# Planned durations of attention and recurrence steps corrected in a build-time instruction order, and one gate scale moved from GpSimd to ScalarE

## The chip, the cores and the metric

The kernel runs on one core of one Trainium2 chip. The metric is the device time of one execution in microseconds (us). Before the change three runs took 2851.94 to 2858.27 us, with a median of 2855.22 us. The engines are named as in the profile: PE is TensorE (PEld its weight loads), DVE is VectorE, ACT is ScalarE, POOL is GpSimd, SP is SyncE, which issues the DMAs.

## The reference

One layer of an encoder works on 2048 tokens of 1024 features, all in float32. What it computes, cut short:

```python
xn   = rms_norm(x, mix_norm_g)
aq, ak, av, mq, mk, mv, mo, ipre, fpre, ga, gm = split(xn @ w_in)
att  = chunk_band_attention(aq, ak, av, rel_bias)   # 8 heads of 64, own chunk of 64 + 8 before
mq, mk = silu(causal_conv4(mq, mk))
hm   = mlstm_chunkwise(mq, mk, mv, ipre + b_i, fpre + b_f)   # 4 heads of 128
hm   = rms_norm(hm per head) * mh_norm_g
m    = sigmoid(mo) * hm
y    = sigmoid(ga) * (att @ w_att_proj) + sigmoid(gm) * (m @ w_mlstm_proj)
x    = x + y @ w_out
x    = x + square(relu(rms_norm(x, ffn_norm_g) @ w_up)) @ w_down
out  = rms_norm(x, final_norm_g)
```

In attention each row of scores is a softmax over at most 640 keys; the recurrence is an mLSTM with exponential input gates, a running maximum and a normalising denominator.

## The kernel before

**Arithmetic.** A float32 product is made of three matmuls in the fp32r format: every operand is split into a rounded part and a rest (`split`, L960 on; weights in `split_now`, L423 on), and high x high, high x low and low x high are added up in PSUM (`mm3`, L486 on). A split is one ACT copy and one DVE subtraction, so each 128x512 activation tile and each 128x1024 weight tile costs both engines a pass. Large products are also done by a seven-product scheme on 2x2 blocks (`quad` at L549, with sums made beforehand by `sum_w` and `quad_w` and combined by `combine`, L1756 on).

**Stages.** The tokens are four blocks of 512. Blocks 0 and 1 come first, one after the other: projections, attention and recurrence are interleaved with the dense matmuls (`dense`, L632 on). Then one gate and the output projection of blocks 0 and 1 and the input projections of blocks 2 and 3 are made in the seven-product scheme. Attention and recurrence of blocks 2 and 3 (`attention_far`, `recurrence_far`) run beside the end of the first feed-forward's up projection and its down projection (`down`, L605 on), whose tiles `take_u1` (L2116) loads from DRAM and splits. `project` (L747) is put ahead of the fourth (for block 2) and of the seventh (for block 3) of the down projection's seven products: it waits until all eight mixing tiles of its block are there.

**The program order.** The order of instructions is not written by hand. Every piece of work is a Python generator, a thread of the class `Flow` (L95 on). Before it issues an instruction it yields the engine and a planned duration in ns; `Flow.run` keeps a planned clock for each engine and always takes the ready thread that can start first, at a tie the one of higher priority. A planned end of a step sets the engine's clock and, with a latency by pair of engines (`LAT`), when the thread's next step may be planned. A third value, where there is one, is added to the time of the result and not to the clock of the engine. A matmul step of any thread but the dense one is planned 800 ns (`SLACK`) after its operands. Buffers (PSUM banks, probability tiles, operand tiles) are handed out by the same planned times. The order that comes out is fixed: on the chip each engine runs its list in order, and waits on semaphores where an operand isn't there. The planned durations change nothing in any instruction; they change which one comes next.

The planned durations are formulas of the width:

```python
def act_ns(n, ps=False, ap=0):
    return (51 if ps else 93) + 0.834 * n + 93 * ap
def dve_ns(n):
    return 70 + 1.042 * n
def dve2_ns(n):
    return 70 + 0.55 * n
```

**The steps that the change touches.** In `scores` (L1243 on), for 128 queries of one head: the score matmuls (L1255) in two halves of up to 320 keys; for each half a DVE pass that adds the bias, negates and keeps the row minimum (L1261, followed by a read of the accumulator); a 128x1 minimum of the two (L1267); Exp with row sum on ACT (L1270, again with a read of its accumulator); a reciprocal (L1272); and the scaling of the probabilities, on DVE (L1275), or in blocks 2 and 3 on ACT (L1277) if that engine can start first. `turn` (L1280 on) transposes the probabilities (L1289) and splits them (L1292 on ACT, L1294 on DVE); `weigh` multiplies them by the values (L1220) and stores them in the block's mixing tiles (L1230 to L1239). In `gates_rest` seven steps of a running maximum over 128 positions (L1395). In `rec_out` the row sum of squares for the head norm (L1665). In `evac_og` (blocks 0 and 1) a Tanh of the output gate on ACT (L1544) and then (tanh + 1) times half the head's gain on POOL (L1547). Blocks 2 and 3 already do the latter on ACT (L1950). POOL also sets the two masked corners of each bias tile (L1149, L1150) and takes the -1/2 powers of the norms (L1621).

Of the kernel before, what the change touches and what calls it, by code (L numbers as in the profile page):

```python
# [26 lines left out]
AF = mybir.ActivationFunctionType  # L27
ALU = mybir.AluOpType
# [66 lines left out]
class Flow:  # L95
# [7 lines left out]
               act=dict(pe=220.0, act=130.0, dve=130.0, pool=180.0),  # L103
               dve=dict(pe=220.0, act=130.0, dve=130.0, pool=155.0), pool=dict(pe=290.0, act=130.0, dve=60.0),
# [68 lines left out]
    def run(self):  # L173
        while self.ready or self.blocked:
            moved = True
            while moved:
                moved = False
                for th in sorted(self.blocked, key=lambda x: (x.prio, x.n)):
                    ok, value = self._grant(th)
                    if ok:  # L180
                        self.blocked.remove(th)
                        self.now = th.at
                        self._step(th, value)
                        moved = True
            if not self.ready and not self.blocked:
                break
            if not self.ready:
                raise RuntimeError("no thread can go on")
            best = None
            for th in self.ready:  # L190
                t, frm = th.at
                for e in th.req[0].split("|"):
                    prio = th.prio
                    if e[-1] == "!":
                        e, prio = e[:-1], -1
                    start = t + self.LAT[frm].get(e, 0.0)
                    if e == "pe" and th.prio < 5:
                        start += self.SLACK
                    key = (max(self.clock[e], start), prio, th.n)
                    if best is None or key < best[0]:  # L200
                        best = (key, th, e)
            (start, _, _), th, e = best
            self.ready.remove(th)
            end = start + th.req[1]
            self.clock[e] = end
            if len(th.req) > 2:
                end += th.req[2]
            th.at = self.now = (end, e)
            self._step(th, e)
# [12 lines that stand above are left out]
# [3 lines left out]
class Layer:  # L225
# [1017 lines left out]
    def scores(self, b, i, k, q, bias, sct, ev):  # L1243
        fl, nc = self.fl, self.nc
        e, st = sct
        f = 4 if b == 0 else i
        n = (i + 5 - f) * P
        kf = k.rearrange("p a c -> p (a c)")
        halves = 2 if n > 256 else 1
        w = n // halves  # L1250
        bks = yield "get", self.banks, halves
        yield "pe", 500
        for x in range(halves):
            for y in range(2):
                nc.tensor.matmul(bks[x][:, :w], q[:, y, i * P:(i + 1) * P],  # L1255
                                 kf[:, f * P + x * w:f * P + x * w + w], start=y == 0, stop=y == 1)
        br = bias[:, ::-1]
        j0 = 640 - n
        for x in range(halves):
            yield "dve", dve_ns(w)  # L1260
            nc.vector.tensor_tensor_reduce(  # L1261
                out=e[:, x * w:x * w + w], in0=bks[x][:, :w], in1=br[:, j0 + x * w:j0 + x * w + w],
                op0=ALU.add, op1=ALU.min, scale=-1.0, scalar=3e38, accum_out=st[:, x:x + 1])
            fl.put(self.banks, bks[x])
        if halves == 2:
            yield "dve", 75
            nc.vector.tensor_tensor(st[:, 0:1], st[:, 0:1], st[:, 1:2], op=ALU.min)  # L1267
        mx = st[:, 0:1]
        yield "act", act_ns(n, ap=2)
        nc.scalar.activation(e[:, :n], e[:, :n], AF.Exp, scale=-1.0, bias=mx, accum_out=st[:, 2:3])  # L1270
        yield "dve", 75
        nc.vector.reciprocal(st[:, 3:4], st[:, 2:3])  # L1272
        e0 = yield ("act|dve" if b > 1 else "dve"), 60 + dve2_ns(n)
        if e0 == "dve":
            nc.vector.tensor_scalar(e[:, :n], e[:, :n], st[:, 3:4], None, op0=ALU.mult)  # L1275
        else:
            nc.scalar.mul(e[:, :n], e[:, :n], st[:, 3:4])  # L1277
        fl.set(ev)
# [69 lines left out]
    def gates_rest(self, b, bk):  # L1348
        fl, nc, B, sm = self.fl, self.nc, self.blk[b], self.sm
# [8 lines left out]
        e, d, s, s2, p = (sm[n] for n in ("e", "d", "s", "s2", "p"))  # L1358
# [32 lines left out]
        V.tensor_copy(a[:, 64:], bk[:16, 128:256])  # L1391
        sh = 1
        while sh < P:
            yield "dve", 150
            V.tensor_tensor(z[:, 64:], a[:, 64:], a[:, 64 - sh:192 - sh], op=ALU.max)  # L1395
            a, z = z, a
            sh *= 2
# [3 lines left out]
                         start=True, stop=True)  # L1401
# [137 lines left out]
    def evac_og(self, b, h, bk):  # L1539
        fl, nc, B = self.fl, self.nc, self.blk[b]  # L1540
        yield "wait", [B["ctx_ev"][h]]
        dst = B["ctx"][h][2][:, :512]
        yield "act", act_ns(512, True)
        nc.scalar.activation(dst, bk, AF.Tanh, scale=0.5)  # L1544
        fl.put_dense(self.banks, bk)
        yield "pool", 670
        nc.gpsimd.tensor_scalar(dst, dst, 1.0, self.ghead[:, h:h + 1], op0=ALU.add, op1=ALU.mult)  # L1547
        fl.set(B["og_ev"][h])

    def rec_head(self, b, h):  # L1550
# [105 lines left out]
    def rec_out(self, n, bk, nd, hs, c, ev):  # L1656
        fl, nc = self.fl, self.nc
        yield "act", act_ns(129, True, 1)
        nc.scalar.mul(nd, bk[:, 260:389], self.ex[:, 1, n:n + 1])
        yield "dve", dve_ns(129)  # L1660
        nc.vector.tensor_add(nd, bk[:, 0:129], nd)
        fl.put(self.banks, bk)
        (tmp,) = yield "get", self.temp, 1
        yield "act", act_ns(128, False, 1)
        nc.scalar.activation(tmp[:, :P], nd[:, :P], AF.Square, accum_out=hs[:, 2, c:c + 1])  # L1665
        fl.put(self.temp, tmp)
        fl.set(ev)
# [793 lines left out]
```

## Time and profile before

| what | value |
|---|---|
| median of 3 runs | 2855.22 us |
| the profiled execution | 2851.86 us |
| its span, first to last instruction | 2850.1 us |
| PE busy | 2806.0 us (98%) |
| DVE busy | 2022.0 us (71%) |
| ACT busy | 1579.1 us (55%) |
| POOL busy | 47.3 us (2%) |
| chain that ended last | PE 81%, DVE 7%, DMA 5%, ACT 4% |

The profile is of one execution. A row of a group names the line of the code, the engine, the operation, the tiles written and read, the shapes and the count; after the bar come busy us, the mean ns of one, and the idle time of the engine before them with what ended it. A row of waits says who waited for whom, with the sum in us, the times and the longest. A row of a stretch gives the busy time of PE, PEld, DVE, ACT and POOL (with counts), the granted clock, and the DMA share and rate. The end of a matmul is modelled and lies after the start of the next one, so PE reads as busy for some time in which it could already have started another.

### The profile page before, as it was taken

The numbers are of one execution on the slowest core, as the hardware profiler recorded it, in microseconds if no ns is written. First come the engines' busy times: TensorE is split into PE (matmuls) and PEld (weight loads), VectorE is DVE, ScalarE is ACT, GpSimd is POOL, SyncE is SP. The second block draws the span as 40 slices with busy tenths as digits, with TensorE's granted clock in tenths as the row PEclk, the third lists the DMA queues.
The fourth block names the chain that finished last, engine by engine and source line by source line (L and its number), as shares of the span: only waits on it lengthen the run. The fifth ranks groups of instructions, "written<-read, shape, count | busy, mean of one in ns | idle before, by whom it ended". The sixth has DMA issues, their size and how long they took to land.

```text
span 2850.1 us, 39045 instructions
## 1 busy us (share of the span) xinstructions
PE 2806.0 (98%) x13576; PEld 2343.9 (82%) x13576; DVE 2022.0 (71%) x3750; ACT 1579.1 (55%) x2734; POOL 47.3 (2%) x116
## 2 busy tenths in 40 slices
PE   8999999999999999999999999999999999999998
PEld 7888888888878888878888887888878888888887
DVE  6886479878896867865666787788886744455565
ACT  4664366755444545665456776566545655555444
POOL 0000000000000000000000000000000000000000
PEclk9999999999999999999999999999999999999999
DMA  6327732357765768487888866866677655566563
GB/s 215 99 93 253 247 110 92 119 201 244 258 214 193 237 231 295 165 270 270 299 283 277 257 210 192 242 194 207 222 259 257 211 198 195 200 235 213 187 224 134
DMA packets 276005, 605.74 MB, mean 213 GB/s; under 512 B 30688, under 2 KB 45152, under 8 KB 275808
## 3 DMA queue, kind: packets, MB, share of 16 engines
q1 hardware_dynamic: 275808, 603.26, 63.1%
q8 instruction: 106, 1.74, 0.2%
q14 instruction: 91, 0.75, 0.1%
HBM read 426.98 MB, written 176.16 MB: 212 GB/s over the span
## 4 chain that ended last, share of the span: by engine, by line
PE 81%; DVE 7%; DMA 5%; ACT 4%; issue 1%; POOL 0%; SPq 0%; POOLq 0%; DVEq 0%; ACTq 0%
PE bank L571 36%; PE bank L488 11%; PE bank L489 11%; PE bank L490 11%; PE bank L599 2%; DMA r<-u 2%; PE bank L1220 2%; DVE wsp L429 2%; PE bank L1255 1%; PE bank L1289 1%; ACT wsp L427 1%; DMA wsum<-ctx 1%; DMA ctx<-in_wf 1%; ACT r L963 1%; DVE r L1294 1%
## 5 line engine op out<-in xcount | busy, mean ns | idle before, releaser
L571 PE MATMUL bank<-r,wsp 128*128 128x512 f32 x5208 | 1189.9, 390 | 8.3 <-DVE ctx L1775 6.8
L571 PEld LDWEIGHTS bank<-r,wsp 128*128 128x128 f32 x5208 | 976.9, 188 | 214.3 <-DVE ctx L1775 9.0
L429 DVE TENSOR_TENSOR wsp<-wraw,wsp 128x1024 fp32r<-128x1024 f32 x461 | 562.9, 1221 | 343.0 <-ACT wsp L427 326.1
L427 ACT CAST wsp<-wraw 128x1024 fp32r<-128x1024 f32 x461 | 484.2, 1051 | 464.4 <-PE bank L571 186.9
L488 PE MATMUL bank<-r,wsp 128*128 128x512 f32 x1600 | 640.4, 400 | 0.9 <-ACT r L1237 0.5
L490 PE MATMUL bank<-r,wsp 128*128 128x512 f32 x1600 | 625.1, 391 | 0.0
L489 PE MATMUL bank<-r,wsp 128*128 128x512 f32 x1600 | 624.7, 390 | 0.0
L490 PEld LDWEIGHTS bank<-r,wsp 128*128 128x128 f32 x1600 | 300.3, 188 | 64.8
L488 PEld LDWEIGHTS bank<-r,wsp 128*128 128x128 f32 x1600 | 301.0, 188 | 53.3 <-ACT r L1237 1.0
L489 PEld LDWEIGHTS bank<-r,wsp 128*128 128x128 f32 x1600 | 301.3, 188 | 51.4
L1775 DVE TENSOR_TENSOR ctx<-bank,ctx 128x512 f32<-128x512 f32 x174 | 118.9, 687 | 86.9 <-PE bank L571 86.9
L968 DVE TENSOR_TENSOR r<-r 128x512 fp32r<-128x512 f32 x224 | 149.7, 687 | 37.1 <-ACT r L963 36.1
L963 ACT CAST r<-r 128x512 fp32r<-128x512 f32 x224 | 136.7, 622 | 69.2 <-DMA r<-u 65.4
L1767 ACT COPY ctx<-bank 128x512 f32<-128x512 f32 x174 | 101.1, 582 | 67.7 <-PE bank L571 61.3
L1270 ACT ACTIVATE sc<-sc,scs 128x640 f32<-128x640 f32 (+4 forms) x128 | 97.2, 760 | 70.9 <-DVE scs L1267 68.5
L396 DVE TENSOR_TENSOR ctx<-ctx,ctx 128x512 f32<-128x512 f32 x112 | 76.7, 688 | 70.7 <-DMA ctx<-in_wf 55.5
L2134 ACT ACTIVATE ctx<-ctx 128x512 f32<-128x512 f32 x96 | 60.6, 632 | 107.4 <-DVE ctx L1775 107.1
L1261 DVE CUSTOM_DVE_ANT_0 sc<-bank,bias 128x320 f32<-128x320 f32 (+3 forms) x240 | 104.9, 459 | 15.6 <-PE bank L1255 12.8
L1220 PE MATMUL bank<-r,r 128*128 128x256 f32 (+1 forms) x672 | 110.5, 285 | 5.5 <-DVE r L1294 4.3
L1220 PEld LDWEIGHTS bank<-r,r 128*128 128x128 f32 x672 | 99.2, 191 | 18.8 <-DVE r L1294 9.0
L1294 DVE TENSOR_TENSOR r<-bank,r 128x512 fp32r<-128x512 f32 (+1 forms) x168 | 96.0, 594 | 12.4 <-ACT r L1292 11.6
L1292 ACT CAST r<-bank 128x512 fp32r<-128x512 f32 (+1 forms) x168 | 81.1, 517 | 14.7 <-PE bank L1289 12.8
(276 smaller groups left out, 2888.9 us busy)
## 6 DMA issues: line engine op xcount, KB each, us to landing
wraw<-in_wf SPq DMA_DIRECT2D x170, 512.0 KB, 4.2
wraw<-wsum SPq DMA_DIRECT2D x136, 512.0 KB, 4.0
r<-u SPq DMA_DIRECT2D x224, 256.0 KB, 3.9
wraw<-in_w SPq DMA_DIRECT2D x104, 512.0 KB, 3.9
u<-ctx SPq DMA_DIRECT2D x128, 256.0 KB, 2.6
ctx<-in_wf SPq DMA_DIRECT2D x112, 256.0 KB, 4.3
wsum<-ctx SPq DMA_DIRECT2D x112, 256.0 KB, 3.7
u<-tmp SPq DMA_DIRECT2D x96, 256.0 KB, 3.2
```

Source lines behind the costliest of these rows:

```text
L427: nc.scalar.copy(w[:, 0], raw)
L429: nc.vector.tensor_sub(w[:, 1], raw, w[:, 0].bitcast(F32))
L488: mm(ps, lh, rh, start=first, stop=False)
L489: mm(ps, lh, rl, start=False, stop=False)
L490: mm(ps, ll, rh, start=False, stop=last)
L571: mm(ps, wv[:, x, k, n], a[:, y], start=new and k == 0 and x == y == 0, stop=k == 3 and x == 1, skip_group_check=True)
L963: self.nc.scalar.copy(dst[:, 0], src)
L968: self.nc.vector.tensor_sub(dst[:, 1], src, dst[:, 0].bitcast(F32))
L1220: nc.tensor.matmul(bk[:, c0:c0 + w], st, sl[:, x, o:o + w], start=n == 0, stop=n == total - 1)
L1261: nc.vector.tensor_tensor_reduce(out=e[:, x * w:x * w + w], in0=bks[x][:, :w], in1=br[:, j0 + x * w:j0 + x * w + w], op0=ALU.add, op1=ALU. ...
L1294: nc.vector.tensor_sub(slot[:, 1, :o], bk[:, :o], slot[:, 0, :o].bitcast(F32))
L1775: nc.vector.tensor_add(t[:, o:o + 512], ps, t[:, o:o + 512])
```

## The change

Five planned durations become longer, one planned duration becomes a choice by engine, and one instruction goes from POOL to ACT:

- score pass on DVE (L1261): 85 ns more for each half;
- Exp (L1270): 25 ns more on ACT's clock, and 90 ns more until its result;
- scaling of the probabilities: a dictionary by engine, 60 + `dve2_ns(n)` on DVE as before, `act_ns(n, ap=1)` on ACT; `Flow.run` reads it;
- running maximum (L1395): 195 ns in place of 150;
- row sum of squares in the recurrence (L1665): 100 ns more;
- output gate of blocks 0 and 1: the scale is an ACT instruction with scale and bias columns, of the same value.

```diff
-            end = start + th.req[1]
+            end = start + (th.req[1][e] if isinstance(th.req[1], dict) else th.req[1])
...
-            yield "dve", dve_ns(w)
+            yield "dve", dve_ns(w) + 85
...
-        yield "act", act_ns(n, ap=2)
+        yield "act", act_ns(n, ap=2) + 25, 90
         nc.scalar.activation(e[:, :n], e[:, :n], AF.Exp, scale=-1.0, bias=mx, accum_out=st[:, 2:3])
...
-        e0 = yield ("act|dve" if b > 1 else "dve"), 60 + dve2_ns(n)
+        cost = dict(act=act_ns(n, ap=1), dve=60 + dve2_ns(n))
+        e0 = yield ("act|dve" if b > 1 else "dve"), cost
...
-            yield "dve", 150
+            yield "dve", 195
             V.tensor_tensor(z[:, 64:], a[:, 64:], a[:, 64 - sh:192 - sh], op=ALU.max)
...
-        yield "pool", 670
-        nc.gpsimd.tensor_scalar(dst, dst, 1.0, self.ghead[:, h:h + 1], op0=ALU.add, op1=ALU.mult)
+        yield "act", act_ns(512, False, 2)
+        g = self.ghead[:, h:h + 1]
+        nc.scalar.activation(dst, dst, AF.Identity, scale=g, bias=g)
...
-        yield "act", act_ns(128, False, 1)
+        yield "act", act_ns(128, False, 1) + 100
         nc.scalar.activation(tmp[:, :P], nd[:, :P], AF.Square, accum_out=hs[:, 2, c:c + 1])
```

## Prediction

> **What bounds the kernel now.** I read the page first, then the busy times by stretch, then PE's waits in the stretches where attention and the recurrence run, then the chain of work in the worst of them.
>
> ```profile
> span 2850.1 us, 39045 instructions
> ...
> PE 2806.0 (98%) x13576; PEld 2343.9 (82%) x13576; DVE 2022.0 (71%) x3750; ACT 1579.1 (55%) x2734; POOL 47.3 (2%) x116
> ```
>
> PE sets the time. The change removes no matmul, so it can only win or lose in the 2850.1 - 2806.0 = 44.1 us in which PE has nothing to do. The stretches show where these lie (PE's busy time is the first number after the length, DVE's the third, ACT's the fourth):
>
> ```profile
> 60.00:260.00 200.00, 197.93 (x1083) 167.50 (x1083) 158.16 (x446) 128.12 (x298) 10.45 (x24) 1.00 0.37 124
> 370.00:580.00 210.00, 208.67 (x1214) 182.64 (x1213) 174.65 (x476) 147.07 (x336) 12.59 (x21) 1.00 0.35 115
> 1200.00:1400.00 200.00, 193.08 (x841) 158.15 (x840) 136.80 (x178) 116.27 (x176) 0.00 (x0) 0.99 0.79 272
> 1550.00:2050.00 500.00, 489.08 (x2740) 419.95 (x2740) 400.34 (x1012) 320.45 (x670) 13.19 (x43) 1.00 0.70 218
> ```
>
> The first two and the last are attention and recurrence of block 0, of block 1, and of blocks 2 and 3. PE is idle there for 2.07, 1.33 and 10.92 us, 14.3 us together. The third row has no step that the change touches; its 6.92 us are shown because a shifted order could reach them. The rest of the 44.1 us lies at the start, the end and in other stages. So the best that better planning in the three stretches can bring is 14.3 us, and a little more: a recorded matmul covers part of each wait.
>
> ```profile
> 1761.04 0.39 PE L489 MATMUL bank<-r,wsp 128*128 128x512 f32 x1
> 1761.27 0.39 PE L490 MATMUL bank<-r,wsp 128*128 128x512 f32 x1
> 1761.50 1.25 PE L1289 MATMUL bank<-const,sc 128*128 128x128 f32 x10
> ...
> 1764.84 0.55 PE L1289 MATMUL bank<-const,sc 128*128 128x128 f32 x3 [1.64 <-ACT sc L1277]
> 1766.26 0.39 PE L1220 MATMUL bank<-r,r 128*128 128x256 f32 x1 [0.88 <-ACT r L1292]
> ...
> 1771.91 0.47 PE L488 MATMUL bank<-r,wsp 128*128 128x512 f32 x1
> ```
>
> Dense matmuls start 0.23 us apart and are recorded 0.39 long, so each wait costs about 0.39 - 0.23 = 0.16 us more than its record. With some two dozen waits in the three stretches that is about 4 us (an estimate): 18 us, or 0.6% of the span, is the ceiling. The same rows show a drain: from 1761.50 to 1771.91, 10.4 us, no dense matmul runs, because `project` waits for block 2's last mixing tile and only attention's own steps are left.
>
> Who releases PE in the last stretch:
>
> ```profile
> PE bank L1220 <- DVE r L1294: 2.6, 4, 1.0
> PE bank L1289 <- ACT sc L1277: 2.0, 2, 1.6
> ...
> PE bank L1220 <- ACT r L1292: 0.9, 1, 0.9
> PE bank L1255 <- DVE scs L1261: 0.8, 1, 0.8
> ...
> PE bank L1289 <- DVE scs L1261: 0.5, 1, 0.5
> ...
> PE bank L488 <- DVE scs L1261: 0.2, 1, 0.2
> ```
>
> L1277 and L1261 are steps whose planned time the change corrects: 2.0 + 0.8 + 0.5 + 0.2 = 3.5 us. The chain says how they come about, and what else is behind them:
>
> ```profile
> 1758.81 3.61 DMA r<-u
> ...
> 1763.02 1.04 ACT wsp L427
> 1764.06 0.73 ACT sc L1277
> 1764.79 0.81 ACT sc L1270 x2
> 1765.60 0.02 issue
> 1765.62 0.59 ACT r L1292
> ```
>
> A load of `u` lands late, ACT's list stands behind its split (L963), and then a weight copy, a scaling and an Exp stand in a row before the copy that PE needs.
>
> **The change part by part.** The rows of each operation:
>
> ```profile
> L1261 DVE CUSTOM_DVE_ANT_0 sc<-bank,bias 128x320 f32<-128x320 f32 x192 | 88.1, 482 | 15.6 <-PE bank L1255 12.8 <-issue 2.2
> L1261 DVE DVE_READ_ACCUMULATOR2_ANT scs<- 128x1 f32 x240 | 19.3, 80 | 0.0
> L1270 ACT ACTIVATE sc<-sc,scs 128x640 f32<-128x640 f32 x96 | 79.4, 827 | 58.0 <-DVE scs L1267 57.9
> L1270 ACT ACTIVATION_READ_ACCUMULATOR sc<-sc,scs 128x1 f32 x128 | 24.0, 187 | 0.0
> L1277 ACT ACTIVATE sc<-sc,scs 128x640 f32<-128x640 f32 x33 | 27.3, 831 | 5.6 <-DVE scs L1272 4.3 <-DVE scs L1267 1.2
> L1395 DVE TENSOR_TENSOR cum<-cum 16x128 f32<-16x128 f32 x28 | 7.8, 277 | 0.7
> L1665 ACT ACTIVATE tmp<-ctx 128x128 f32<-128x128 f32 x64 | 19.9, 311 | 19.2 <-DVE ctx L1661 17.3 <-DVE tmp L797 1.6
> ```
>
> *Scaling on ACT.* Planned 60 + 70 + 0.55 x 640 = 482 ns whichever engine takes it; now 93 + 0.834 x 640 + 93 = 720 on ACT. In the chain it holds ACT for 0.73 us. This is the one large error of the old list: 238 ns each, 33 times, 7.9 us of ACT that the plan did not know of. I expect most of the gain from it.
>
> *Exp.* Planned 813 on ACT's clock for 640 columns, now 838, and its result 90 later, at 928. In the chain Exp and accumulator read hold ACT for 0.81, which is the old figure; the old plan then allowed 130 for the way to DVE. The new one counts the readback and the way.
>
> *Score pass.* A half of 320 columns was planned 70 + 1.042 x 320 = 403, now 488. The record is 482 long with a read of 80 behind it, but DVE is not held so long:
>
> ```profile
> 1626.14 0.40 DVE sc L1261
> 1626.54 0.01 DVE scs L1261
> ```
>
> The next instruction starts after 0.41. So 488 is right for the result and 78 ns too long for the engine: 240 x 78 = 19 us of DVE that the plan now sees and the chip doesn't have.
>
> *Running maximum and row sum.* 28 x 45 = 1.3 us and 64 x 100 = 6.4 us more of plan; the 277 of L1395 is still above 195, and L1665's 311 and its read stand against 393. No instruction changes.
>
> *Gate scale.* Eight POOL instructions go, eight of ACT come. The trace has the same ACT instruction for blocks 2 and 3:
>
> ```profile
> L1950 ACT ACTIVATE ctx<-ctx,ghead 128x512 f32<-128x512 f32 x8 | 6.5, 811 | 0.0
> L1547 POOL TENSOR_SCALAR ctx<-ctx,ghead 128x512 f32<-128x512 f32 x8 | 9.9, 1232 | 42.5 <-ACT ctx L1544 42.1
> L1275 DVE TENSOR_SCALAR sc<-sc,scs x95: 271/547/707, 79.5 to 2014.7; 128x640 f32<-128x640 f32 x63, 128x128 f32<-128x128 f32 x8, 128x256 f32<-128x256 f32 x8, 128x384 f32<-128x384 f32 x8
> ```
>
> ACT gets 8 x 0.81 = 6.5 us in two stretches where it is idle for 72 and 63 us; four instructions in each. Whoever is queued behind one on ACT, a transposed copy (L1292) above all, is 0.8 us late at most if ACT was full just then, and PE waits for that copy. Bounds: 0 and 6.5 us; I take 0.3, because only 3.4 us of PE idle time is found there at all. The operand comes from ACT's own Tanh (L1544), so no engine waits for a new partner. POOL's list gets shorter; the tile is read much later (L1640), so nothing waits for the step itself, now or then.
>
> The longest L1275 is 707 ns against a median of 547. If that is POOL's doing, 0.16 us of DVE comes back for each such meeting; I take 0.2 us for all eight. [...]
>
> **The sum.** Waits of PE released by corrected steps: 3.5 us, and 5 x 0.16 = 0.8 that the records cover; the copy behind Exp at 1766.26, 0.9 + 0.16: 5.4 us in all, which I take away whole, because the list will place these matmuls after the corrected time plus its 800 ns. Of the other 14.3 - 4.4 = 9.9 us, released by L1294 and others, I take a quarter, 2.5 us: these steps stand in the same queues behind the corrected ones, but late loads of `u` stay. Gate: + 0.3 - 0.2. Sum: -5.4 - 2.5 + 0.1 = -7.8 us. The bounds are -18 (every wait gone) and the first rival's price on the other side. From the profiled execution, 2851.86 us (span 2850.1 and 1.8 around it), that is 2844.1; that execution lies 3.36 us below the median of 2855.22, so the forecast is **2847 us**.
>
> **The rivals.**
>
> *The plan gets too slow, and the drain grows (slower).* The list is made later for attention than the chip is. In block 2 the plan adds 64 x 85 = 5.4 us on DVE, 32 x 115 = 3.7 us in Exp, and half of 7.9 = 3.9 us in scaling: 13 us, of which half in series, since two units of scores are in flight. Attention's matmuls are placed 6.5 us later among the dense ones, but the dense ones still stop at `project`. So up to 6.5 us more of attention is left for the drain at 1761.50, with PE waiting for chains of ACT and DVE. It decides as soon as the plan's delay exceeds the waits saved. For it: that drain exists and ends with block 2's last tile. Against: half of the drain is PE's own work, and a later place also means fewer waits before. All of it, with nothing gained elsewhere: 2855.2 + 6.5 = 2862.
>
> *The waits only move.* Three waits of the last stretch start at a load of `u`, as the one above and these:
>
> ```profile
> 1578.76 5.00 DMA r<-u
> ...
> 1740.01 4.34 DMA r<-u
> ...
> r<-u SPq DMA_DIRECT2D x224, 256.0 KB, 3.9
> ```
>
> The list plans 900 ns on SP and 2000 to the landing; the row says 3.9 us. The change leaves that as it is. If these loads are the true cause, the order changes and the idle time doesn't: 2855, between 2850 and 2860.
>
> *Another stage takes up the shift.* The 6.9 us of the stretch from 1200 are waits for sums whose operands come by DMA; if the shifted plan issues those loads in another order, they can double: 2862.
>
> **How the numbers follow.** The forecast has a chance of 0.42 (own range 2840 to 2849), waits that only move 0.22, the larger drain 0.28, another stage 0.08. A measurement of this kernel can tell about 0.2%, 5.7 us, from no change (2849.5 to 2860.9). So faster 0.42, same 0.22, slower 0.36. The range goes from 2840, a saving of 15 of the 18 us, to 2867, where the first and third rival each have most of their price.
>
> **What would show it.** Right: PE's waits for L1277 and L1261 from 1550 to 2050 gone, PE idle there under 6 us, the drain no longer than 10.4 us, ACT with eight more instructions of 0.81 before 580 and PE's idle time there within 1 us of 3.4. Wrong: a stretch without dense matmuls before block 2's `project` of 13 us or more; waits of the same sum under other names behind loads of `u`; or PE idle time that grows in 1200 to 1400, where no step was touched.

## The result and the profile after

The changed kernel takes 2861.05 us (median of 14 runs, 2854.49 to 2864.51) where the kernel before takes 2855.31 us (14 runs). The ratio is 1.0016, 95% interval [1.0009, 1.0023]: 0.16% or 4.6 us slower (the two medians lie 5.7 us apart). I had forecast 2847 us, faster. The time lies inside the range, on the other side of the kernel before.

From here on "the change" is the whole diff. The line numbers after it are one higher from L1274 and two higher from L1548: L1277 is now L1278, L1289 is L1290, L1292 is L1293, L1294 is L1295.

The page of the changed kernel, span and engines:

```profile
span 2855.8 us, 39034 instructions
...
PE 2810.0 (98%) x13576; PEld 2347.9 (82%) x13576; DVE 2020.3 (71%) x3745; ACT 1587.9 (56%) x2747; POOL 38.1 (1%) x108
```

The work on PE is the same 13576 matmuls, the span is 5.7 us longer. Only 1.7 us of that is more idle time of PE (44.1 to 45.8 us); its recorded busy time grew by 4.0 us. The stretches of the changed kernel (us from the start, length, busy time of PE, PEld, DVE, ACT, POOL), then one stretch of the kernel before that was not shown yet:

```profile
60.00:260.00 200.00, 196.30 (x1072) 165.59 (x1071) 157.68 (x443) 131.06 (x303) 6.36 (x20) 1.00 0.38 123
370.00:580.00 210.00, 208.10 (x1211) 180.97 (x1210) 172.78 (x475) 146.44 (x332) 7.72 (x17) 1.00 0.34 109
1200.00:1400.00 200.00, 194.82 (x849) 159.92 (x848) 138.16 (x180) 118.80 (x180) 0.00 (x0) 0.99 0.79 269
1550.00:2050.00 500.00, 489.94 (x2745) 422.27 (x2743) 398.19 (x1008) 323.08 (x674) 13.52 (x43) 0.99 0.71 219
2050.00:2230.00 180.00, 172.66 (x781) 143.05 (x781) 130.36 (x185) 93.06 (x138) 2.70 (x2) 0.98 0.76 250
```

```profile
2050.00:2230.00 180.00, 174.50 (x798) 144.25 (x798) 133.94 (x189) 95.07 (x143) 2.70 (x2) 1.00 0.75 253
```

PE's idle time grew in block 0 from 2.07 to 3.70 us and in block 1 from 1.33 to 1.90, fell in the far stage from 10.92 to 10.06, and went from 5.50 to 7.34 in 2050 to 2230. That last stretch must not be counted as a gain or a loss of the order: its matmuls stand in the same order in both kernels, and its row has a granted clock of 0.98 in place of 1.00 (more on this in the last section). I laid the lists of the two traces beside each other, by line and shape: in PE, DVE, ACT and the DMA issues the order differs only between about 50 and 300, 350 and 750, and 1550 and 2110 us. (Of the 13576 matmuls 2814 stand elsewhere, nearly all between 50 and 620 and between 1550 and 2070.) The stretch from 750 to 1550 and the end from 2110 on have the same instructions in the same order.

A stretch given in us from the start shifts with what came before it. For the comparison of many runs I therefore take a part from the start of one numbered matmul to the start of another, the same numbers in every run: no. 233 to 1493 (block 0, 60 to 300 us in the kernel before), 1809 to 3198 (block 1, 370 to 620), 7253 to 8604 (far stage up to block 2's projection, 1545 to 1790) and 8604 to 9986 (to the end of block 3, 1790 to 2045). These four are "the parts" below.

The waits of PE in the far stage of the changed kernel (1550 to 2050), the longest:

```profile
PE bank L1220 <- ACT r L1293: 2.0, 1, 2.0
PE bank L1290 <- DVE scs L1261: 1.8, 2, 1.5
PE bank L1220 <- ACT r L963: 1.7, 1, 1.7
PE bank L1220 <- DVE r L1295: 1.4, 4, 0.4
PE bank L1255 <- DVE r L1295: 0.8, 1, 0.8
PE bank L1255 <- DVE scs L1261: 0.7, 1, 0.7
```

The 2.0 us for the scaling are gone, as I said they would be. But the score pass (L1261) now has 1.8 + 0.7 us in place of 1.5, the copy behind Exp 2.0 in place of 0.9, and a wait of 1.7 us for the split of a tile of `u` (L963) is new. The drain ahead of block 2's projection, in PE's order of time:

```profile
1760.99 0.39 PE L490 MATMUL bank<-r,wsp 128*128 128x512 f32 x1
1761.22 1.03 PE L1290 MATMUL bank<-const,sc 128*128 128x128 f32 x8
...
1768.30 0.58 PE L1220 MATMUL bank<-r,r 128*128 128x256 f32 x1 [1.96 <-ACT r L1293]
1769.33 1.11 PE L1220 MATMUL bank<-r,r 128*128 128x256 f32 x4 [0.45 <-DVE r L1295]
1770.24 0.73 PE L488 MATMUL bank<-r,wsp 128*128 128x512 f32 x1
```

It is no longer than before (1761.22 to 1770.24, 9.0 us against 10.4). The largest wait, 1.96 us, starts in the chain at a load of `u` once more:

```profile
1760.49 5.84 DMA r<-u
...
1766.36 0.62 ACT r L963
```

In block 0 PE's waits are these, first before and then after (60 to 262 us):

```profile
PE bank L1220 <- DVE r L1294: 1.7, 4, 0.9
PE bank L1599 <- DVE ctx L1583: 0.2, 1, 0.2
```

```profile
PE bank L1220 <- DVE r L1295: 2.9, 7, 0.7
PE bank L1220 <- ACT r L1293: 0.3, 1, 0.3
PE bank L1603 <- DVE cst L1606: 0.3, 1, 0.3
```

The probability tiles now come late seven times, not four. Here are the two rows of the gate part, the new instruction on ACT and the scaling on DVE:

```profile
L1549 ACT ACTIVATE ctx<-ctx,ghead x8: 801/816/832, 99.7 to 550.9; 128x512 f32<-128x512 f32 x8
L1276 DVE TENSOR_SCALAR sc<-sc,scs x91: 278/545/556, 80.1 to 1988.7; 128x640 f32<-128x640 f32 x59, 128x128 f32<-128x128 f32 x8, 128x256 f32<-128x256 f32 x8, 128x384 f32<-128x384 f32 x8
```

One gate instruction holds ACT for 0.816 us, as priced, and the longest scaling on DVE falls from 707 to 556 ns. The one of 707 ns ran from 404.8 us on, while POOL had its step (404.0 to 405.2).

### The profile page after: what moved, and what is told of

Its sections match the earlier page's. It is cut to its first block, busy times and chain, and to the rows that moved or that the text cites. A ratio compares the mean times of both kernels' runs of the same rounds, so it can differ in the third digit from the quotient of the medians.

```text
span 2855.8 us, 39034 instructions
## 1 busy us (share of the span) xinstructions
PE 2810.0 (98%) x13576; PEld 2347.9 (82%) x13576; DVE 2020.3 (71%) x3745; ACT 1587.9 (56%) x2747; POOL 38.1 (1%) x108
## 4 chain that ended last, share of the span: by engine, by line
PE 81%; DVE 7%; DMA 7%; ACT 3%; issue 1%; SPq 0%; POOL 0%; POOLq 0%; DVEq 0%; ACTq 0%
PE bank L571 37%; PE bank L488 11%; PE bank L489 11%; PE bank L490 11%; PE bank L599 2%; PE bank L1220 2%; PE bank L1255 2%; DMA r<-u 2%; DVE wsp L429 1%; PE bank L1290 1%; DMA ctx<-in_wf 1%; DMA wsum<-ctx 1%; DVE r L968 1%; ACT wsp L427 1%; DVE sc L1261 1%
## 5 line engine op out<-in xcount | busy, mean ns | idle before, releaser
L571 PE MATMUL bank<-r,wsp 128*128 128x512 f32 x5208 | 1192.2, 390 | 8.4 <-DVE ctx L1777 5.2
L571 PEld LDWEIGHTS bank<-r,wsp 128*128 128x128 f32 x5208 | 978.9, 188 | 214.3 <-DVE ctx L1777 6.9
L963 ACT CAST r<-r 128x512 fp32r<-128x512 f32 x224 | 136.4, 622 | 67.9 <-DMA r<-u 60.0
L1270 ACT ACTIVATE sc<-sc,scs 128x640 f32<-128x640 f32 (+4 forms) x128 | 97.4, 761 | 64.0 <-DVE scs L1267 60.8
L1261 DVE CUSTOM_DVE_ANT_0 sc<-bank,bias 128x320 f32<-128x320 f32 (+3 forms) x240 | 104.9, 459 | 11.0 <-PE bank L1255 7.8
L1295 DVE TENSOR_TENSOR r<-bank,r 128x512 fp32r<-128x512 f32 (+1 forms) x168 | 96.7, 594 | 14.8 <-ACT r L1293 13.9
L1293 ACT CAST r<-bank 128x512 fp32r<-128x512 f32 (+1 forms) x168 | 82.5, 514 | 16.4 <-PE bank L1290 12.2
```

Of the source, the lines that this page charges most:

```text
L571: mm(ps, wv[:, x, k, n], a[:, y], start=new and k == 0 and x == y == 0, stop=k == 3 and x == 1, skip_group_check=True)
L963: self.nc.scalar.copy(dst[:, 0], src)
L1261: nc.vector.tensor_tensor_reduce(out=e[:, x * w:x * w + w], in0=bks[x][:, :w], in1=br[:, j0 + x * w:j0 + x * w + w], op0=ALU.add, op1=ALU. ...
```

## The experiments

Two theories stood at the start: the gate's instruction costs, or the new order that the longer durations give. A third came up on the way: the durations mean nothing in themselves, and any edit draws another order out of the list, good or bad by a few us. All ratios are to the kernel before, run beside it on the same chip; its median there lay between 2853.09 and 2856.97 us, so the medians of two rows can't be compared directly. The parts are in us, from one profile each.

| run | median us | ratio, 95% interval | block 0 | block 1 | far, block 2 | far, block 3 |
|---|---|---|---|---|---|---|
| before | 2855.31 | 1 | 239.9 | 250.0 | 244.9 | 255.0 |
| the change | 2861.05 | 1.0016 [1.0009, 1.0023] | 242.6 | 251.0 | 246.3 | 252.3 |
| e1_swap | 2857.24 | 1.0000 [0.9991, 1.0010] | 240.7 | 249.8 | 244.2 | 255.1 |
| e2_gate | 2853.80 | 0.9996 [0.9986, 1.0006] | 241.9 | 249.7 | 245.4 | 255.1 |
| e3_costs | 2860.33 | 1.0011 [1.0000, 1.0022] | 243.2 | 252.0 | 247.1 | 252.8 |
| e4_score | 2859.51 | 1.0010 [1.0002, 1.0019] | 242.3 | 252.2 | 253.6 | 251.3 |
| e13_exp | 2854.17 | 0.9995 [0.9983, 1.0008] | 242.0 | 252.8 | 242.6 | 255.8 |
| e14_square | 2848.94 | 0.9979 [0.9970, 0.9988] | 239.9 | 250.9 | 242.0 | 252.3 |
| e15_scale | 2855.68 | 0.9998 [0.9989, 1.0006] | 240.1 | 250.1 | 246.3 | 250.8 |
| e16_scan | 2856.64 | 1.0004 [0.9995, 1.0013] | 240.0 | 249.9 | 244.1 | 260.6 |
| e5_rest | 2867.73 | 1.0046 [1.0032, 1.0060] | 243.7 | 255.2 | 243.4 | 257.1 |
| e6_result | 2853.54 | 0.9992 [0.9981, 1.0003] | 243.4 | 249.8 | 247.0 | 248.5 |
| e7_u | 2860.97 | 1.0024 [1.0012, 1.0035] | 242.6 | 250.8 | 251.8 | 254.0 |
| e8_null | 2849.73 | 0.9980 [0.9971, 0.9988] | 240.1 | 250.0 | 244.7 | 249.3 |
| e9_after76 | 2859.27 | 1.0016 [1.0007, 1.0024] | 242.1 | 251.1 | 253.2 | 249.4 |
| e10_after74 | 2860.60 | 1.0014 [1.0005, 1.0024] | 241.7 | 250.7 | 246.7 | 256.7 |
| e11_before78 | 2857.07 | 1.0012 [1.0001, 1.0023] | 240.5 | 249.9 | 249.5 | 252.0 |
| e12_before83 | 2853.97 | 0.9998 [0.9988, 1.0008] | 241.5 | 249.8 | 243.7 | 255.5 |
| e17_scale_late | 2872.56 | 1.0073 [1.0059, 1.0087] | | | | |
| e18_late | 2862.14 | 1.0035 [1.0021, 1.0048] | | | | |

Before, e1_swap and e2_gate have the same order of matmuls in the far stage; their parts there agree within 1.2 us. In block 0 before and e1_swap have the same order too and differ by 0.8 us. Differences of that size say nothing, and a profile of one run can be further off: that of e4_score is of the slowest of its 11 runs (2866.67 us), that of e16_scan of one 5 us above its median.

**Which half of the change.** e1_swap issues the gate's scale on ACT but plans it as the POOL step it was, so the list of every other engine stays:

```diff
         yield "pool", 670
-        nc.gpsimd.tensor_scalar(dst, dst, 1.0, self.ghead[:, h:h + 1], op0=ALU.add, op1=ALU.mult)
+        g = self.ghead[:, h:h + 1]
+        nc.scalar.activation(dst, dst, AF.Identity, scale=g, bias=g)
```

> Only the instruction moves: the gate scale of blocks 0 and 1 is issued on ScalarE, but the list plans it as the 670 ns GpSimd step it was, so every other engine keeps the order of the kernel before. Theory 'the ScalarE instruction costs': eight instructions of 0.81 us in two stretches delay the copies that TensorE waits for; +2 to +4 us, with more TensorE idle from 60 to 260 and 370 to 580 us. Rival 'the cost is in the new order': within 1 us of the kernel before, TensorE idle in these stretches as before (2.07 and 1.33 us).

e2_gate is the gate part of the diff as it stands.

> The gate part of the change alone, planned and issued on ScalarE; all other planned durations as before. Theory 'the gate part costs': +3 to +6 us, the whole of the change's +5.7, out of the first two blocks. Rival 'the planned durations cost': at most +2 us here, and the rest with the durations.

e3_costs is the diff without the gate part:

```diff
-        yield "act", act_ns(512, False, 2)
-        g = self.ghead[:, h:h + 1]
-        nc.scalar.activation(dst, dst, AF.Identity, scale=g, bias=g)
+        yield "pool", 670
+        nc.gpsimd.tensor_scalar(dst, dst, 1.0, self.ghead[:, h:h + 1], op0=ALU.add, op1=ALU.mult)
```

> The five planned durations and the choice by engine alone; the gate scale stays on GpSimd. Theory 'the planned durations cost': +4 to +6 us. Rival 'the gate part costs': within 2 us of the kernel before. If my forecast's mechanism works and only the gate part spoils it: 2 to 6 us faster than before.

The gate's instruction costs nothing that can be measured (1.0000 and 0.9996); the durations alone give +0.11%, with an interval from 1.0000 on. My price of 0.3 us for the gate is not contradicted, though intervals of 0.09% to 0.10% either way, some 2.7 us, can't confirm it either. In block 0 the change is no longer than e3_costs, which has the same order there and no gate part (242.6 and 243.2 us), so the loss of block 0 lies in the order.

**Which duration.** e4_score, e13_exp, e14_square, e15_scale and e16_scan each have one of the five, all else as before; e5_rest has four of them, without the score pass:

```diff
-            yield "dve", dve_ns(w)
+            yield "dve", dve_ns(w) + 85
```

> Only the score pass is planned 85 ns longer for each half; nothing else is changed. Theory 'the plan counts VectorE time that the chip does not spend' (78 ns for each of 240 halves): +3 to +6 us, the larger part of the change, with the stretch without dense matmuls before block 2's projection as long as in the changed kernel or longer. Rival 'no single duration matters': within 2 us of before.

The score pass alone is 0.10% slower. Block 2's part of the far stage is 8.7 us longer in the trace, and PE's list shows a long drain there:

```profile
1762.57 0.39 PE L490 MATMUL bank<-r,wsp 128*128 128x512 f32 x1
1762.80 0.64 PE L1220 MATMUL bank<-r,r 128*128 128x256 f32 x4
...
1785.56 0.59 PE L488 MATMUL bank<-r,wsp 128*128 128x512 f32 x1
```

From 1762.80 to 1785.56 no dense matmul runs, 22.8 us. This is my first rival, and it exists: a plan that is later for attention than the chip is leaves more of it for the drain. Block 3's part gives 3.7 us of it back. As the profile is of the slowest run, 8.7 us is more than the order costs in the median.

e5_rest against the kernel before, cut short:

```diff
-        yield "act", act_ns(n, ap=2)
+        yield "act", act_ns(n, ap=2) + 25, 90
...
-            yield "dve", 150
+            yield "dve", 195
...
-        e0 = yield ("act|dve" if b > 1 else "dve"), 60 + dve2_ns(n)
+        cost = dict(act=act_ns(n, ap=1), dve=60 + dve2_ns(n))
+        e0 = yield ("act|dve" if b > 1 else "dve"), cost
...
-        yield "act", act_ns(128, False, 1)
+        yield "act", act_ns(128, False, 1) + 100
```

> The complement of the run with the score pass alone: Exp, scaling, running maximum and row sum are planned as in the change; the score pass and the gate scale are as before. Theory 'padding' (the score pass's 85 ns count VectorE time that the chip does not spend, and this is what costs): 1 to 4 us faster than before. Theory 'any other order costs' (the order of before is a lucky draw among many): +2 to +5 us.

Four of the five together are 0.46% slower, worse than all five (1.0011 without the gate). So "the score pass's padding costs" cannot be the whole cause, and the edits do not add up: 0.10% for the score pass and 0.46% for the others would be 0.56%, and together they give 0.11%.

> Only Exp is planned longer (25 ns of ScalarE and 90 ns to the result). Theory 'longer durations in the chain of scores cost in blocks 0 and 1': block 0 +2 to +4 us, block 1 +1 to +5, in all +3 to +10 us. Rival 'it is the sum of the edits, none alone': within 2 us in both blocks, the far stage anywhere within 6 us of before.

> Only the row sum of squares of the recurrence is planned 100 ns longer. Theory 'the chain of scores': blocks 0 and 1 within 1 us of before, in all -4 to +4 us. Rival 'the recurrence's steps': block 1 +3 to +5 us, as in the run with the four others together.

> Only the scaling of the probabilities is planned at its ScalarE time, 720 ns in place of 482, in blocks 2 and 3. My forecast's main term: TensorE's waits for the scaling (2.0 us) gone and 2 to 4 us saved in the far stage. Theory 'the order there is a draw': -6 to +6 us, blocks 0 and 1 within 1 us of before as nothing of theirs is changed.

> Only the seven steps of the running maximum are planned at 195 ns in place of 150. Theory 'the order is a draw': -4 to +4 us; blocks 0 and 1 within 1.5 us of before, since the scan is over before the first score pass of each. Rival 'the recurrence's steps cost': block 1 +3 us or more.

Exp alone lengthens blocks 0 and 1 by 2.1 and 2.8 us, as expected of the chain of scores; the far stage gives only 1.5 us of it back in the profile, and yet the time is 0.9995, not the 3 to 10 us more that this theory gave. The row sum alone leaves block 0 as it is and has the lowest median of the study: 0.9979, 6 us better than before, a little beyond what I had allowed it. Running maximum alone: no difference. The sum of the five alone and the gate alone is +0.10 - 0.05 - 0.21 - 0.02 + 0.04 - 0.04 = -0.18%; all six together are +0.16%. (Each of the six has an interval of about 0.1% either way, so the pair of complements above is the stronger evidence.)

The scaling was the step from which I expected most. Alone it saves nothing (0.9998), and PE's waits for it (L1278 here) grew, from 2.0 us before to 4.6 (1550 to 2050):

```profile
PE bank L1290 <- ACT sc L1278: 4.6, 5, 2.7
PE bank L1220 <- DVE r L1295: 1.7, 3, 0.9
```

3.5 of the 4.6 us lie in the drain, from the second of these rows to the last:

```profile
1767.45 0.39 PE L490 MATMUL bank<-r,wsp 128*128 128x512 f32 x1
1767.68 0.60 PE L1255 MATMUL bank<-r,r 128*128 128x320 f32 x3
...
1784.30 0.45 PE L488 MATMUL bank<-r,wsp 128*128 128x512 f32 x1
```

**Time of the result in place of time of the engine.** e6_result is the change with the score pass's 85 ns in the third place, so that they delay the result and not DVE's next instruction, which is what the trace of before showed (0.41 us until the next one):

```diff
-            yield "dve", dve_ns(w) + 85
+            yield "dve", dve_ns(w), 85
```

> The changed kernel, but the score pass's 85 ns are added to the time of its result and not to VectorE's clock. Theory 'padding': the loss goes, within 2 us of before or faster. Theory 'any other order costs': +2 to +6 us, like the changed kernel.

The loss goes: 0.9992. On its face this bears out the padding. But block 0 is not better than in the change (243.4), and the gain comes from block 1 and block 3, so it may as well be another draw; the next runs say how much one is worth.

**Loads of `u`.** e7_u plans the landing of the change's `u` loads at 3600 ns after the issue:

```diff
-        yield "sp", 900, 2000
+        yield "sp", 900, 3600
         self.nc.sync.dma_start(r[:, 1].bitcast(F32), src)
```

> The changed kernel with the loads of u planned to land 3600 ns after their issue in place of 2000. Theory 'late loads of u are the cause of the waits in the far stage': 3 to 6 us faster than the changed kernel, 0 to 2 us faster than before, with no wait of TensorE in that stage that goes back to a load of u. Theory 'any other order costs': +2 to +6 us over before, with such waits moved elsewhere.

1.0024: that theory falls. The loads stand at the start of single waits, but a plan that is nearer to what they take (4.2 us in the median in the change, 3.9 before) is not better.

**Orders for nothing.** e8_null, e11_before78 and e12_before83 are the kernel before with 1, 3 and 8 ns more on the planned reciprocal; e9_after76 and e10_after74 are the change with 1 ns more and less. No instruction differs from the kernel each starts from.

```diff
-        yield "dve", 75
+        yield "dve", 76
         nc.vector.reciprocal(st[:, 3:4], st[:, 2:3])
```

> The kernel before with one planned duration longer by 1 ns (the reciprocal after Exp, 76 in place of 75): nothing that the plan could know better. Theory 'padding': within 2 us of before. Theory 'any other order costs': +2 to +5 us, as much as the change itself, with block 0 and block 1 each 1 us or more longer in the trace.

> The changed kernel with 1 ns more on the planned reciprocal (76). Theory 'the order is a draw' (any small edit gives another order of attention's steps, and orders differ by several us for no reason that a planned duration tells): anywhere from -5 to +12 us over before, and not like the changed kernel's +4.6 except by chance. Rival 'the longer durations cost, in any order': +3 to +7 us, with block 0 (1083 matmuls from 60 to 300 us) 2 to 3 us longer than before, as in every run with longer durations so far.

> The changed kernel with 1 ns less on the planned reciprocal (74). As for the 76: the draw gives anything from -5 to +12 us over before; 'longer durations cost' gives +3 to +7 us, with block 0 longer by 2 to 3 us.

> The kernel before with 3 ns more on the planned reciprocal (78). 'The order is a draw': -6 to +10 us, with stages of attention that differ by several us from before. 'Longer durations cost': -5 to +2 us, with block 0 within 1 us of before.

> The kernel before with 8 ns more on the planned reciprocal (83). 'The order is a draw': -6 to +10 us, and not near the run with 78 except by chance. 'Longer durations cost': -5 to +2 us, with block 0 within 1 us of before.

One ns on a 75 ns step gives 0.20% (0.9980), 3 ns lose 0.12% (an interval from 1.0001 on), 8 ns change nothing. So several us can be won, and perhaps some lost, without telling the plan anything. The stretches of the run with 1 ns more say where the gain is:

```profile
60.00:260.00 200.00, 197.88 (x1082) 167.40 (x1082) 158.47 (x447) 127.92 (x298) 10.48 (x24) 1.00 0.38 124
370.00:580.00 210.00, 208.63 (x1214) 182.64 (x1213) 174.46 (x475) 146.53 (x335) 12.57 (x21) 1.00 0.37 115
1550.00:2050.00 500.00, 492.89 (x2763) 425.61 (x2762) 402.07 (x1016) 321.71 (x673) 15.05 (x44) 0.99 0.71 219
```

Blocks 0 and 1 are as before; in the far stage PE is idle 7.11 us in place of 10.92.

The two neighbours of the change take what the change takes (1.0016 and 1.0014). I had set this down as what "longer durations cost" expects, and it looks like it. But their lists say otherwise: beside the change, e9_after76 has no matmul elsewhere before 1650 us, and e10_after74 only a few, between 447 and 453 us. In blocks 0 and 1 they are the same draw as the change, not new ones. What is new, the far stage, spreads: 246.3 + 252.3, 253.2 + 249.4 and 246.7 + 256.7 us. And the run with 8 ns more, whose block 0 does have another order, loses 1.6 us there as well. So before's order of block 0 was better than the others tried, by 1.6 to 3.8 us (but for e11_before78, whose 0.6 us is less than e1_swap shows with before's own order), for reasons that no single duration carries.

**The drain.** e18_late is the kernel before with block 2's projection one product later, e17_scale_late the same with the scaling's duration:

```diff
-PROJ = {2: (3, 0), 3: (6, 0)}
+PROJ = {2: (4, 0), 3: (6, 0)}
```

> Scaling alone at its ScalarE time, and block 2's projection ahead of the fifth product in place of the fourth. Theory 'the waits belong to the drain': the stretch without dense matmuls (16.8 us with the scaling alone) falls under 4 us, TensorE's waits for the scaling from 4.6 to under 1 us, and the two far parts together are 2 to 6 us shorter. Rival 'errors of the plan': the waits stay, and the time is that of the scaling alone within 2 us.

> The kernel before with block 2's projection ahead of the fifth product in place of the fourth, all durations as before. Theory 'the waits belong to the drain': no stretch of over 4 us without dense matmuls before that projection, and 2 to 6 us saved, unless a second drain ahead of block 3's projection takes it back. Rival 'errors of the plan': waits for the scaling and for the copy behind Exp of about 2.5 us stay at other places; within 2 us of before.

Both are slower (1.0073 and 1.0035), and the drain did not go but moved, to block 3's projection. For e18_late, its edges in PE's list and PE's longest wait from 1550 to 2070:

```profile
2001.91 0.40 PE L490 MATMUL bank<-r,wsp 128*128 128x512 f32 x1
2002.14 0.38 PE L1289 MATMUL bank<-const,sc 128*128 128x128 f32 x2
...
2056.93 0.40 PE L488 MATMUL bank<-r,wsp 128*128 128x512 f32 x1
```

```profile
PE bank L1289 <- ACT sc L1277: 5.7, 3, 2.8
```

and for e17_scale_late, the same wait and the two stretches:

```profile
PE bank L1290 <- ACT sc L1278: 11.3, 5, 3.1
```

```profile
1550.00:1800.00 250.00, 247.66 (x1399) 213.06 (x1398) 196.57 (x520) 165.23 (x356) 8.31 (x26) 1.00 0.71 221
1800.00:2070.00 270.00, 247.60 (x1337) 210.57 (x1336) 206.78 (x498) 153.11 (x314) 6.00 (x18) 0.97 0.65 209
```

There are now 54.8 us without dense matmuls in e18_late. Where the drain was, up to 1800, PE is idle only 2.34 us in e17_scale_late; where it went, 22.4. In the kernel before the two stretches have 6.89 and 4.04 us of idle time (with the scaling alone 6.76 and 1.79):

```profile
1550.00:1800.00 250.00, 243.11 (x1373) 209.48 (x1373) 197.72 (x531) 161.77 (x349) 8.29 (x27) 0.99 0.71 223
1800.00:2070.00 270.00, 265.96 (x1466) 227.29 (x1465) 214.09 (x498) 165.41 (x330) 6.21 (x17) 1.00 0.70 217
```

The waits for the scaling went with the drain (all 5.7 and 11.3 us lie in it) and grew with its length, with the old duration and with the new one. So they belong to the drain. My hope of a gain from the later place was wrong by the clause that I had put in: a second drain took back more than the first had cost.

## Why the prediction was wrong

**What held.** PE sets the time (busy for 98% of the span in both profiles). The price of the gate, 0.1 us in sum, is compatible with 1.0000 and 0.9996. Taking the step off POOL freed next to nothing on DVE, as I had taken it: 707 ns fell to 556 on the longest scaling, 0.15 us. The drain ahead of block 2's projection exists, and its length differs with the order (10.4 us before, 9.0 in the change, 22.8 with the score pass alone). Of my signs of being right, the waits for L1277 are gone and the drain is no longer; but PE is idle for 10.06 us from 1550 to 2050, not under 6, and for 5.60 us in blocks 0 and 1, not within 1 us of 3.4. Of my signs of being wrong, waits under other names came, two of them behind loads of `u`.

**The step that failed** is "5.4 us in all, which I take away whole, because the list will place these matmuls after the corrected time plus its 800 ns". It rests on taking a wait whose releaser is a corrected step for an error of the plan. The largest of them stood in the drain. There PE has only attention's chain to run, so a longer planned duration can't put other work ahead of the matmul. The scaling's own run bears this out (waits 2.0 to 4.6 us, time 0.9998), and the two runs that moved the drain show that the waits move with it. In the change the two waits of that name are gone and others stand in the same place: 1.96 us for the copy behind Exp, at the end of a load of `u`. That was the mechanism of my second rival, "the waits only move"; its time, 2855 and at most 2860, was not met.

**The second term** of the sum, a quarter of the other waits or -2.5 us, had no ground that the runs bear out: PE's idle time from 1550 to 2050 fell by 0.86 us in all, where the two terms together had asked for about 6.

**What was not in the sum at all** is a cost in blocks 0 and 1: +2.7 and +1.0 us in the change. I saw 3.4 us of idle time there as something to gain, and took it as the bound. It is a bound on the gain alone. Another order can have more, and nearly all that were tried in block 0 did. Of the 2.7 us most is waits for probability tiles (1.7 to 2.9 us recorded, and, by the forecast's estimate of 0.39 - 0.23, 0.16 more for each of three new ones). The third rival had the right idea in the wrong place: the shift reached no stage that the change does not touch, since the lists from about 760 to 1550 are the same, and PE's idle time from 1200 to 1400 fell from 6.92 to 5.18 us.

**A premise that failed** is "it can only win or lose in the 2850.1 - 2806.0 = 44.1 us in which PE has nothing to do". Of the 5.7 us of span 4.0 are recorded as busy, with the same matmuls. Part of that goes with a lower granted clock (0.996 over the profiled span, 0.998 before; last section), for which the sum had no term. The four parts, +2.7, +1.0, +1.4 and -2.7 us, come to +2.4 only.

**The first rival** gave a price of 6.5 us for a longer drain. The change's drain is not longer, so it does not explain the result. In the score pass alone it is 22.8 us long, and that part took 8.7 us more in the profile of its slowest run. But a long drain alone does not decide: with the scaling alone it is 16.6 us, at 0.9998.

**What is shown and what stays open.** Shown: the gate's instruction has no cost that can be measured; the durations' effects do not add up; the order alone moves the time, as 1 ns on a step, with no instruction changed, moves it by as much as the whole change. Argued, not shown: that the change has no mean effect of its own beyond the draw. Three neighbours of the kernel before lie at -0.20, +0.12 and -0.02%, the change at +0.16%; with so few independent orders a true loss of 0.1% from the longer durations can't be told from a draw. What makes one order of block 0 better than another was not found either: waits for L1294 are the form that the loss takes, not its cause. And part of the loss goes with a lower granted clock (0.9959 in the mean of the runs, 0.9971 before), which no run separates from the order (last section).

Two versions are faster than both kernels: the row sum alone, 2848.94 us, ratio 0.9979 [0.9970, 0.9988], and one ns on the reciprocal, 2849.73 us, 0.9980 [0.9971, 0.9988].

## What to carry to other kernels

Where an order comes from a list scheduler, a planned duration is a seed as much as a measurement: before crediting a correction with a gain or a loss, change something by 1 ns and see how far the time moves on its own. Before a wait is called an error of the plan, see whether the engine had anything else in its list at that place; in the drain here it hadn't, and the corrected duration did not help. And the idle time of a stage bounds what can be won there, not what can be lost: block 0 had 2.07 us of it here, and lost 2.7.

## What the runs showed that I had not expected

Parts with the same order in every run are not equally long. From 1150 to 1400 us in the kernel before, where PE waits for sums whose operands come by DMA (6.8 us in four waits for L1775; the chain to the one that ends at 1310.8 goes through a load `ctx<-in_wf` of 5.16 us), the same matmuls took 245.0 to 252.6 us in the profiles of before, the change and e1 to e16 (250.1 before, 248.2 in the change), and those from 2045 to 2230 took 182.2 to 190.1 (185.1 before, 189.8 in the change). That is over 7 us in either between two profiles with the same order of matmuls there (182.2 in e11_before78, 189.7 in e12_before83), more than the whole result: single profiles of this kernel can be compared by parts, with care, and hardly by span.

In the second of these stretches the granted clock goes with the length, and I had passed over it. Up to PE's last matmul it falls from 1.00 to 0.50 for two pieces of 3.4 us in the profile of the kernel before (at 1272.0 and 1766.9 us) and for five in that of the change (at 1232.0, two in a row from 1767.9, at 2139.9 and 2215.0). In the 10 us ahead of each (of the two in a row, ahead of the first) PE had been idle for 2.2 to 3.4 us; but no piece comes within 10 us after the wait of 1.71 us that starts at 1874.4 in the change. Two neighbouring stretches of the change show it:

```profile
2136.50:2139.90 3.40, 2.38 (x21) 2.27 (x21) 2.36 (x5) 1.33 (x3) 1.01 (x1) 1.00 0.51 165
2139.90:2143.30 3.40, 3.40 (x15) 2.94 (x14) 1.41 (x2) 2.42 (x4) 0.37 (x1) 0.50 0.80 292
```

In such a piece dense matmuls start 0.43 us apart (L571 in the piece at 2215.0) in place of 0.23. From 2045 to 2230 the kernel before has no such piece and took 185.1 us; the change has two and took 189.8. The three pieces more, each 3.4 us at half the clock, can cost up to 5.1 us (an estimate: 3 x 3.4 x 0.5), and the spans differ by 5.7. Over all runs the mean granted clock is 0.9959 in the change (14 runs) and 0.9971 in the kernel before (141 runs beside the experiments); that is worth up to 3.4 us of the 4.6 (an estimate: 0.0012 of 2855). It is not the whole loss, since e10_after74 has 0.9972 and takes 1.0014; and whether the new order's waits bring the pieces about or they fall by chance, no run here shows.
